# Emptying the first bank of a plain group ahead of the next operands' preparation

## The chip, the cores and the metric

The kernel runs on one core of a Trainium2 chip. The metric is the device time of one execution in microseconds (us). The engines are named as in the profile: PE is TensorE (matmuls), DVE VectorE, ACT ScalarE, SP the engine that issues most DMAs.

## What is computed

One decoder block for 256 tokens of width 2048, in fp32: a mixer and a gated feed-forward network, each with an RMSNorm ahead and a residual sum behind. Cut to what matters:

```python
h = rmsnorm(x, mix_norm_w)
q, k, v, g_out, gk_low, gate_b, gate_c, xc, merge_a, merge_b = split(h @ w_in)
o = rmsnorm(gla_chunked(q, k, v, log_g), gla_norm_w)
y_a = o * silu(g_out)
y_b = gate_b * causal_depthwise_conv(gate_c * xc, conv_w)
x = x + (sigmoid(merge_a) * y_a + sigmoid(merge_b) * y_b) @ w_out
gate, up = split(rmsnorm(x, ffn_norm_w) @ w_gate_up)      # hidden width 5632
x = x + (silu(gate) * up) @ w_down
return rmsnorm(x, final_norm_w)
```

Nearly all of the work is in the products with w_in, w_out, w_gate_up and w_down, whose weights are read once.

## The kernel before

**Split products.** PE multiplies in fp32r. A value is split into hi (rounded) and lo (the rest), and a product is three matmuls: lo of the weights with the activations, hi with their low part, hi with hi (`mm3`, lines 347 to 349 of the profile; the weights are the moving operand there, 128 x 512).

**Pieces.** The weights come in pieces of 512 KB, in the order of one list, `stream`. For each piece `load_piece` issues the DMA into `raw` (5 buffers), then `high` (L238, ACT) writes hi (6 buffers). The lo of a piece, `low` (L243, DVE), is written when the next piece is loaded (`finish_low`). `take` is called for each piece before PE uses it, and loads ahead as far as LOOK = 5 pieces beyond those used. Activations (xh and xl, hh and hl, acth and actl) are split in the same way.

**Two kinds of groups.** A pair of products of the same kind, such as fg4 and fu4 (the gate and the up projection of block 4 of the hidden layer) or gc0 and xc0, is made with seven block products in place of eight (`sevens`). It needs sums of weights: t1 (L259, raw<-y,x) and t3, t2 and t4, which change a tile x in place (L265, x<-x,raw or x<-x,y); each then goes to hi on ACT and to lo on DVE. So such a piece is a chain DVE, ACT, DVE, PE. A pair has five PSUM banks, and at its end the sums v2, v3 and u1 are put together from them on DVE (L424 to L437) and the result goes through a silu on ACT (sg, L1059) and a product on DVE (sg, L1062). The last of these, u1 (L437), reads the bank that the pair's last piece has filled.

The other groups are plain (`eights` for g, gb, ma, mb, wo and the blocks of fg and fu that are not in a pair; `down` for dn). A plain group has two banks, one for each half of the tokens (t = 0 and 1), out of a list of three that is called `lent`. When its last piece has been multiplied for t = 0, that bank is emptied: for g by a silu on ACT (ya, L929), for ma and mb by a sigmoid on ACT and a product on DVE, for wo by a sum on DVE (h, L996), for dn by a sum on DVE (h, L1103), for fg by a silu on ACT (sg8, L1059). The next group needs two of three banks, so its second one is the bank that the group before emptied first. Transposes (trb at L597 from the sg tiles, tr at L583 from h) take a bank of the same list.

**The order of the work.** The pieces of a pair and of plain groups are mixed by rules written out by hand (`gates_list`, `hidden_list`), so a plain group ends somewhere in the midst of a pair. On each engine the instructions stand in the order in which a scheduler puts them, which goes by the order of the program and by what an instruction depends on; an engine works its own list from the front to the back.

Of the kernel before, what the change touches and what calls it, by code (L numbers as in the profile page):

```python
# [12 lines left out]
ALU = mybir.AluOpType  # L13
# [55 lines left out]
PARTS = ((0, 3), (3, 6), (6, 9), (9, 11))  # L69
# [107 lines left out]
def stream_list():  # L177

    pieces = [(p[0], p[3]) for p in piece_list()]
    out = [e for e in pieces if e[0][0] in "kqv"] + gates_list() + [e for e in pieces if e[0] == "wo0"]  # L180
    return out + hidden_list() + down_list()
# [3 lines left out]
def block_kernel(ctx, tc, x, xt, cols_in, gkw_in, gku_in, gnw, conv_w, finw, w_in, w_out, w_gu, w_dn, out):  # L185
    nc = tc.nc
# [12 lines left out]
    def bank(shape, name, tag=None):  # L199

        if tag is None:
            tag = f"b{turn['b'] % turn['of']}"
            turn["b"] += 1
        return psum.tile(shape, F32, tag=tag, name=name)
# [11 lines left out]
    LOOK = 5  # L216
    stream = stream_list()
# [6 lines left out]
    count = {"loaded": 0, "used": 0, "tick": 0}  # L224
    pending = []
    held = {}
# [8 lines left out]
    def high(raw, piece, a=0, b=None):  # L235
        hi, n = piece[0], piece[2]
        ks = slice(a, b or n)
        nc.scalar.copy(hi[:, ks, :], raw[:, ks, :])  # L238

    def low(raw, piece, a=0, b=None):  # L240
        hi, lo, n = piece
        ks = slice(a, b or n)
        nc.vector.tensor_tensor(out=lo[:, ks, :], in0=raw[:, ks, :], in1=hi[:, ks, :].bitcast(F32), op=ALU.subtract)  # L243

    def sum_of(pair, what, q):

        one, two = pair
        if what == "21":
            return fetch(one, 4 * q + 2)
        if what == "22":  # L250
            return fetch(two, 4 * q + 2)
        if what == "11":
            held["y"] = fetch(one, 4 * q, held["pool"], "y")
            return held["y"]
        y = held["y"]
        if what == "t1":
            held["x"] = fetch(two, 4 * q, held["pool"], "x")
            raw = wraw.tile([P, 2, 512], F32, tag="raw", name="raw")
            nc.vector.tensor_tensor(out=raw, in0=y, in1=held["x"], op=ALU.add)  # L259
            return raw  # L260
        x = held["x"]
        if halfway and halfway[-1][0] is x:
            finish_low()
        other = y if what == "t2" else fetch(two if what == "t3" else one, 4 * q + 2)
        nc.vector.tensor_tensor(out=x, in0=x, in1=other, op=ALU.add)  # L265
        return x

    def load_piece():


        i = count["loaded"]
        count["loaded"] += 1
        if i < len(stream):
            key, k0 = stream[i]
            if isinstance(k0, tuple):
                n, w = 2, 512
                raw = sum_of(key, *k0)
                step = n
            else:
                mat, j, n, w = index[(key, k0)]  # L280
                raw = wraw.tile([P, n, w], F32, tag="raw", name="raw")

                step = n // 2 if i < 2 else n
            piece = [whi.tile([P, n, w], F32R, tag="hi", name="hi"), None, n]
            if isinstance(k0, tuple):
                high(raw, piece)
                halfway.append((raw, piece, key, k0))
            else:
                if i < 2:
                    piece[1] = wlo.tile([P, n, w], F32R, tag="lo", name="lo")  # L290
                for a in range(0, n, step):
                    b = a + step
                    if (i, a) in hooks:
                        hooks.pop((i, a))()
                    nc.sync.dma_start(
                        raw[:, a:b, :], mats[mat][j, :, a * w:b * w].rearrange("p (k c) -> p k c", c=w))
                    high(raw, piece, a, b)
                    if i < 2:
                        low(raw, piece, a, b)
                if i < 2:  # L300
                    ready[(key, k0)] = piece
                else:
                    halfway.append((raw, piece, key, k0))
        if len(halfway) > 1 or (halfway and i >= len(stream)):
            finish_low()

    def finish_low():
        raw, piece, key, k0 = halfway.pop(0)
        piece[1] = wlo.tile([P, piece[2], PIECE // piece[2]], F32R, tag="lo", name="lo")
        low(raw, piece)  # L310
        ready[(key, k0)] = piece
# [19 lines left out]
    def one_at_a_time(delay, fn):  # L331

        spaced.append((count["tick"] + delay, fn))

    def take(key, k0):
        while count["loaded"] <= len(stream) and count["loaded"] <= count["used"] + LOOK:
            load_piece()
        return ready.pop((key, k0))

    def used(n=1):  # L340
        count["used"] += n
        for _ in range(n):
            tick()
# [7 lines left out]
    def tok_piece(ps, t, piece, k0, first, last, a):  # L351
        hi, lo, n = piece
        for k in range(n):
            ah, al = a(t, k0 + k)
            mm3(ps, ah, al, hi[:, k, :], lo[:, k, :], first and k == 0, last and k == n - 1)
# [19 lines left out]
    def eights(key, a, done, tags=None):  # L375

        mine = tags or [lent.pop(0) for _ in range(NT)]
        ps = [bank([P, 512], f"{key}_{t}", tag) for t, tag in enumerate(mine)]
        for k0 in range(0, KC, 2):
            piece, _ = yield  # L380
            for t in range(NT):
                tok_piece(ps[t], t, piece, k0, k0 == 0, k0 == KC - 2, a)

                if k0 == KC - 2:
                    done(t, ps[t])
        if tags is None:
            lent.extend(mine)

# [676 lines left out]
    order = hidden_list()  # L1065
# [17 lines left out]
    def hidden_act(part):  # L1083
        def pair(t, k):
            hi, lo = act_of(PARTS[part][0] + k // 4)
            ts = slice(t * P, (t + 1) * P)
            return hi[:, k % 4, ts], lo[:, k % 4, ts]

        return pair

    def down(key):

        part, n = (int(s) for s in key[2:].split("_"))
        cs = slice(DOWN[part][n][0], sum(DOWN[part][n]))
        mine = [lent.pop(0) for _ in range(NT)]
        ps = [bank([P, cs.stop - cs.start], f"{key}_{t}", tag) for t, tag in enumerate(mine)]
        number = sum(e[0] == key for e in order)
        for i in range(number):
            piece, k0 = yield
            for t in range(NT):  # L1100
                tok_piece(ps[t], t, piece, k0, i == 0, i == number - 1, hidden_act(part))
                if i == number - 1:
                    nc.vector.tensor_tensor(out=h[:, t, cs], in0=ps[t], in1=h[:, t, cs], op=ALU.add)  # L1103
        lent.extend(mine)

    def hidden(key):
# [39 lines left out]
    order = down_list()  # L1146
# [15 lines left out]
    for e in order:  # L1162
        key, k0 = e
# [82 lines left out]
```

## Time and profile before

| what | value |
|---|---|
| median of 3 runs | 1505.06 us (1503.34, 1506.04, 1505.06) |
| profiled execution | 1504.77 us, span 1503.1 us |
| granted clock of TensorE | 0.999 |
| PE busy | 1489.3 us, 99% |
| DVE busy | 1277.8 us, 85% |
| ACT busy | 862.9 us, 57% |
| mean of one lo (L243) and one hi (L238) | 1218 ns and 1047 ns |
| HBM | 235 GB/s over the span |

A row of a timeline has the start in us from the span's start, the duration, the engine, the line, the operation, out<-in with the tiles' names, and behind them, in brackets, how long the engine had been idle before and what released it. A row with x2 or more holds several instructions. The durations of matmuls are modelled, and overlap; their starts tell how they follow each other. The page's groups give busy time, the mean of one, and the idle time before; a row of PE's waits has the total, the number and the longest.

### The profile page before, as it was taken

The page shows a single profiled execution, that of the slowest core. Times are in us where ns is not written, and L with a number is a line of the kernel's source. Part 1 is how long each engine was busy: PE and PEld are TensorE (multiplying, and loading weights), DVE is VectorE, ACT ScalarE, POOL GpSimd, SP SyncE. Part 2 cuts the span into 40 slices and gives each one's busy share as a digit, 9 for nine tenths or more (in the row PEclk, how much of TensorE's full clock was granted, in tenths as well). Part 3 has the DMA queues.
Part 4 walks back from the last instruction along what each step waited for, and adds up shares of the span by engine and source line. Part 5 has one row for each costly group of instructions (what it writes and reads, how often), then busy time and mean ns, then how long its engine had stood idle before and what let it go on. Part 6 is the DMA issues. An engine that isn't in the chain of part 4 may idle for free.

```text
span 1503.1 us, 19369 instructions
## 1 busy us (share of the span) xinstructions
PE 1489.3 (99%) x7064; PEld 1243.9 (83%) x7064; DVE 1277.8 (85%) x1283; ACT 862.9 (57%) x977; POOL 37.9 (3%) x60
## 2 busy tenths in 40 slices
PE   9999999999999999999999999999999999999998
PEld 8989988888888888888888888888888788888887
DVE  6775869979979878966689999999999999999975
ACT  7773546655654654654556756655565556565553
POOL 0030000000000000000000000000000000000000
PEclk9999999999999999999999999999999999999999
DMA  9655557876886977786666777777877778777782
GB/s 354 200 170 179 171 170 265 273 230 232 281 259 235 304 227 252 258 264 209 217 220 214 238 246 251 255 261 220 272 238 239 253 263 269 246 263 231 235 287 94
DMA packets 100127, 358.57 MB, mean 239 GB/s; under 512 B 11492, under 2 KB 11620, under 8 KB 99904
## 3 DMA queue, kind: packets, MB, share of 16 engines
q1 hardware_dynamic: 96656, 346.73, 70.8%
q0 software_dynamic: 2800, 8.89, 2.2%
q10 hardware_dynamic: 576, 1.72, 0.3%
q8 instruction: 55, 0.90, 0.2%
q14 instruction: 40, 0.33, 0.1%
HBM read 351.03 MB, written 2.10 MB: 235 GB/s over the span
## 4 chain that ended last, share of the span: by engine, by line
PE 89%; DVE 5%; issue 3%; ACT 2%; DMA 1%; SPq 0%; DVEq 0%; ACTq 0%
PE fg L347 7%; PE fg L349 7%; PE fg L348 7%; PE dn L347 5%; PE dn L349 5%; PE dn L348 5%; PE gc L347 3%; PE gc L348 3%; PE gc L349 3%; DVE lo L243 3%; PE wo L347 2%; PE v L347 2%; PE v L348 2%; PE gb L347 2%; PE gb L349 2%
## 5 line engine op out<-in xcount | busy, mean ns | idle before, releaser
L243 DVE TENSOR_TENSOR lo<-raw,hi 128x1024 fp32r<-128x1024 f32 (+1 forms) x506 | 612.5, 1218 | 109.1 <-ACT hi L238 28.0
L238 ACT CAST hi<-raw 128x1024 fp32r<-128x1024 f32 (+1 forms) x506 | 523.8, 1047 | 270.8 <-PE gb L349 26.4
L238 ACT CAST hi<-x 128x1024 fp32r<-128x1024 f32 x144 | 151.6, 1053 | 276.2 <-DVE x L265 211.0
L243 DVE TENSOR_TENSOR lo<-x,hi 128x1024 fp32r<-128x1024 f32 x144 | 176.2, 1223 | 36.1 <-ACT hi L238 26.1
L347 PE MATMUL dn<-lo,acth 128*128 128x512 f32 (+1 forms) x368 | 140.8, 383 | 1.8 <-DVE h L1103 1.0
L349 PE MATMUL dn<-hi,acth 128*128 128x512 f32 (+1 forms) x368 | 139.9, 380 | 0.0
L348 PE MATMUL dn<-hi,actl 128*128 128x512 f32 (+1 forms) x368 | 139.8, 380 | 0.0
L265 DVE TENSOR_TENSOR x<-x,raw 128x1024 f32<-128x1024 f32 x96 | 117.1, 1220 | 14.7 <-DMA raw<-in_w_in_dram 9.3
L347 PE MATMUL fg<-lo,hh 128*128 128x512 f32 x288 | 112.4, 390 | 0.0
L348 PE MATMUL fg<-hi,hl 128*128 128x512 f32 x288 | 112.2, 389 | 0.0
L349 PE MATMUL fg<-hi,hh 128*128 128x512 f32 x288 | 112.2, 389 | 0.0
L347 PE MATMUL fg<-lo,sh 128*128 128x512 f32 x256 | 101.0, 395 | 0.0
L348 PE MATMUL fg<-hi,sl 128*128 128x512 f32 x256 | 99.9, 390 | 0.0
L349 PE MATMUL fg<-hi,sh 128*128 128x512 f32 x256 | 99.8, 390 | 0.0
L347 PEld LDWEIGHTS dn<-lo,acth 128*128 128x128 f32 x368 | 69.2, 188 | 16.2 <-DVE h L1103 2.3
L349 PEld LDWEIGHTS dn<-hi,acth 128*128 128x128 f32 x368 | 69.2, 188 | 13.3
L348 PEld LDWEIGHTS dn<-hi,actl 128*128 128x128 f32 x368 | 69.3, 188 | 12.9
L347 PEld LDWEIGHTS fg<-lo,hh 128*128 128x128 f32 x288 | 54.1, 188 | 11.8 <-DVE lo L243 0.5
L349 PEld LDWEIGHTS fg<-hi,hh 128*128 128x128 f32 x288 | 54.1, 188 | 11.2
L348 PEld LDWEIGHTS fg<-hi,hl 128*128 128x128 f32 x288 | 54.1, 188 | 11.1
L243 DVE TENSOR_TENSOR lo<-y,hi 128x1024 fp32r<-128x1024 f32 x48 | 58.5, 1219 | 5.4 <-ACT hi L238 2.4
L259 DVE TENSOR_TENSOR raw<-y,x 128x1024 f32<-128x1024 f32 x48 | 58.6, 1220 | 3.0 <-DMA y<-in_w_in_dram 1.5
(247 smaller groups left out, 3068.1 us busy)
## 6 DMA issues: line engine op xcount, KB each, us to landing
raw<-in_w_in_dram SPq DMA_DIRECT2D x254, 512.0 KB, 4.6
raw<-in_w_gu_dram SPq DMA_DIRECT2D x176, 512.0 KB, 4.4
raw<-in_w_dn_dram SPq DMA_DIRECT2D x88, 512.0 KB, 4.5
x<-in_w_gu_dram SPq DMA_DIRECT2D x32, 512.0 KB, 4.9
y<-in_w_gu_dram SPq DMA_DIRECT2D x32, 512.0 KB, 3.8
raw<-in_w_out_dram SPq DMA_DIRECT2D x32, 512.0 KB, 3.7
y<-in_w_in_dram SPq DMA_DIRECT2D x16, 512.0 KB, 4.2
x<-in_w_in_dram SPq DMA_DIRECT2D x16, 512.0 KB, 4.9
```

Source lines behind the costliest of these rows:

```text
L238: nc.scalar.copy(hi[:, ks, :], raw[:, ks, :])
L243: nc.vector.tensor_tensor(out=lo[:, ks, :], in0=raw[:, ks, :], in1=hi[:, ks, :].bitcast(F32), op=ALU.subtract)
L259: nc.vector.tensor_tensor(out=raw, in0=y, in1=held["x"], op=ALU.add)
L265: nc.vector.tensor_tensor(out=x, in0=x, in1=other, op=ALU.add)
L347: nc.tensor.matmul(ps, lhsT=sh, rhs=ml, start=first, stop=False, skip_group_check=onto)
L348: nc.tensor.matmul(ps, lhsT=sl, rhs=mh, start=False, stop=False, skip_group_check=onto)
L349: nc.tensor.matmul(ps, lhsT=sh, rhs=mh, start=False, stop=last, skip_group_check=onto)
```

## The change

The set `ends` holds the place in the stream of the last piece of each plain group: those whose names begin with g or m, v1, wo1 to wo3, the plain fg and fu, and dn but for the last part. There `take` looks 4 pieces ahead in place of 5, so that the load of one piece, its hi, and the lo or the sums that go with it, come one take later, behind the group's emptying in the program. The emptying itself goes through `emptying`: for t = 0 it notes the last instruction on DVE and the last on ACT that the emptying wrote, and the next `take` puts what it loads after these two on their engines (`tc.issue_after`, which fixes an order of issue, and is no wait). v1 is in the set, but its group has no such emptying: there only the shorter look ahead holds. The DMAs of the piece that is put off go with it. The function `down` has its sum in a small function `added` for that.

```diff
+    ends = {}
+    for i, (key, k0) in enumerate(stream):
+        if not isinstance(key, tuple) and (key[0] in "gm" or key == "v1" or key[:2] in ("wo", "fg", "fu", "dn")):
+            ends[key] = i
+    ends = {i for key, i in ends.items() if key != "wo0" and key[:3] != f"dn{len(PARTS) - 1}"}
+
     def take(key, k0):
-        while count["loaded"] <= len(stream) and count["loaded"] <= count["used"] + LOOK:
-            load_piece()
+        look = LOOK - (count["used"] in ends)
+        with ExitStack() as order:
+            for ins in held.pop("emptied", ()):
+                order.enter_context(tc.issue_after(ins))
+            while count["loaded"] <= len(stream) and count["loaded"] <= count["used"] + look:
+                load_piece()
         return ready.pop((key, k0))
+
+    def emptying(done, t, ps):
+        traced = nc.cur_bb.bb.instructions
+        last = traced[-1]
+        done(t, ps)
+        if t == 0:
+            start = next(k for k in reversed(range(len(traced))) if traced[k] is last) + 1
+            new = {i.engine: i for i in traced[start:]}
+            held["emptied"] = [new[e] for e in (mybir.EngineType.DVE, mybir.EngineType.Activation) if e in new]
...
-                    done(t, ps[t])
+                    emptying(done, t, ps[t])
...
+        def added(t, ps):
+            nc.vector.tensor_tensor(out=h[:, t, cs], in0=ps, in1=h[:, t, cs], op=ALU.add)
...
-                    nc.vector.tensor_tensor(out=h[:, t, cs], in0=ps[t], in1=h[:, t, cs], op=ALU.add)
+                    emptying(added, t, ps[t])
```

The lines below the change move down by 19 to 22: L929 becomes L951, L1103 becomes L1122. Each engine has the same instructions as before; the order differs. In the rows below a tile's name ends in a number, which tells buffers of one name apart.

ScalarE at the end of g2, before: three hi stand ahead of the table load and the two silus that empty the banks of g2.

```order
L238 CAST hi_4528<-raw_4526 128x1024
L238 CAST hi_4545<-raw_4544 128x1024
L238 CAST hi_4560<-raw_4558 128x1024
L929 ACT_TABLE_LOAD
L929 ACTIVATE ya_4570<-g2_0_4309,r1_120 128x512
L929 ACTIVATE ya_4570<-g2_1_4310,r1_120 128x512
L238 CAST hi_4581<-raw_4580 128x1024
```

And there in the changed kernel:

```order
L238 CAST hi_4528<-raw_4526 128x1024
L238 CAST hi_4545<-raw_4544 128x1024
L951 ACT_TABLE_LOAD
L951 ACTIVATE ya_4564<-g2_0_4309,r1_120 128x512
L951 ACTIVATE ya_4564<-g2_1_4310,r1_120 128x512
L238 CAST hi_4576<-raw_4574 128x1024
L238 CAST hi_4581<-raw_4580 128x1024
```

One hi has gone from ahead of the emptying to behind it.

VectorE where the pair fg4 ends and fg5 begins, before (fg4_1 is the pair's bank that is filled last; x_8726 is the tile of sums of fg5):

```order
L243 TENSOR_TENSOR lo_8744<-raw_8728,hi_8730 128x1024
L243 TENSOR_TENSOR lo_8757<-raw_8740,hi_8741 128x1024
L265 TENSOR_TENSOR x_8726<-x_8726,raw_8752 128x1024
L437 TENSOR_TENSOR u1_8777<-fg4_1_8112,v2_8116 128x512
L1062 SCALAR_TENSOR_TENSOR sg7_8110<-u1_8777,r2_6320,sg7_8110 128x512
L243 TENSOR_TENSOR lo_8769<-x_8726,hi_8755 128x1024
```

And in the changed kernel:

```order
L243 TENSOR_TENSOR lo_8744<-raw_8728,hi_8730 128x1024
L459 TENSOR_TENSOR u1_8777<-fg4_1_8112,v2_8116 128x512
L243 TENSOR_TENSOR lo_8757<-raw_8740,hi_8741 128x1024
L265 TENSOR_TENSOR x_8726<-x_8726,raw_8752 128x1024
L1084 SCALAR_TENSOR_TENSOR sg7_8110<-u1_8777,r2_6320,sg7_8110 128x512
L243 TENSOR_TENSOR lo_8769<-x_8726,hi_8755 128x1024
```

u1 has moved up past a lo and the first sum x of fg5; the product sg stays where it was.

VectorE where fg7 ends and fg9 begins, before (x_10761 is the tile of sums of fg9):

```order
L243 TENSOR_TENSOR lo_10767<-y_10749,hi_10751 128x1024
L243 TENSOR_TENSOR lo_10779<-raw_10763,hi_10765 128x1024
L265 TENSOR_TENSOR x_10761<-x_10761,raw_10787 128x1024
L243 TENSOR_TENSOR lo_10792<-raw_10775,hi_10776 128x1024
L243 TENSOR_TENSOR lo_10804<-x_10761,hi_10790 128x1024
L437 TENSOR_TENSOR u1_10812<-fg7_1_10138,v2_10142 128x512
L265 TENSOR_TENSOR x_10761<-x_10761,y_10749 128x1024
L1062 SCALAR_TENSOR_TENSOR sg7_10136<-u1_10812,r2_6320,sg7_10136 128x512
```

And in the changed kernel:

```order
L243 TENSOR_TENSOR lo_10767<-y_10749,hi_10751 128x1024
L243 TENSOR_TENSOR lo_10779<-raw_10763,hi_10765 128x1024
L459 TENSOR_TENSOR u1_10812<-fg7_1_10138,v2_10142 128x512
L1084 SCALAR_TENSOR_TENSOR sg7_10136<-u1_10812,r2_6320,sg7_10136 128x512
L243 TENSOR_TENSOR lo_10792<-raw_10775,hi_10776 128x1024
L265 TENSOR_TENSOR x_10761<-x_10761,raw_10787 128x1024
L622 TENSOR_TENSOR actl_10729<-trb_10866,acth_10728 128x4x128
L243 TENSOR_TENSOR lo_10804<-x_10761,hi_10790 128x1024
```

u1, the product sg behind it, the lo of a plain piece and an actl now stand ahead of the lo that belongs to the first sum of fg9; u1, sg and that plain lo also stand ahead of the sum itself.

## Prediction

> **What bounds the kernel now.** I read the page first: busy time, then the groups.
>
> ```profile
> PE 1489.3 (99%) x7064; PEld 1243.9 (83%) x7064; DVE 1277.8 (85%) x1283; ACT 862.9 (57%) x977; POOL 37.9 (3%) x60
> L243 DVE TENSOR_TENSOR lo<-raw,hi 128x1024 fp32r<-128x1024 f32 (+1 forms) x506 | 612.5, 1218 | 109.1 <-ACT hi L238 28.0
> L265 DVE TENSOR_TENSOR x<-x,raw 128x1024 f32<-128x1024 f32 x96 | 117.1, 1220 | 14.7 <-DMA raw<-in_w_in_dram 9.3
> ```
>
> PE is the bound, and only a pause of PE can be won or added. DVE is second, at 85%: it has little room to catch up in the stretches where a pair of products makes its sums (x, L265) beside the lo of every piece. Then the waits of PE:
>
> ```profile
> PE dn L347 <- DVE h L1103: 1.0, 2, 0.5
> PE ma L347 <- ACT ya L929: 0.6, 1, 0.6
> ```
>
> None of PE's waits is larger than some 1 us, and these two are what the change is about: the next group's bank is emptied too late. PE's timeline gives their true size, since starts, not the modelled ends, tell what a pause costs:
>
> ```profile
> 510.46 0.39 PE L348 MATMUL ma<-hi,xl 128*128 128x512 f32 x1
> 510.69 0.39 PE L349 MATMUL ma<-hi,xh 128*128 128x512 f32 x1
> 511.71 0.50 PE L347 MATMUL ma<-lo,xh 128*128 128x512 f32 x1 [0.64 <-ACT ya L929]
> 512.05 0.40 PE L348 MATMUL ma<-hi,xl 128*128 128x512 f32 x1
> ...
> 1173.75 0.39 PE L349 MATMUL dn<-hi,acth 128*128 128x512 f32 x1
> 1174.64 0.50 PE L347 MATMUL dn<-lo,acth 128*128 128x512 f32 x1 [0.50 <-DVE h L1103]
> ...
> 1419.81 0.39 PE L349 MATMUL dn<-hi,acth 128*128 128x512 f32 x1
> 1420.65 0.50 PE L347 MATMUL dn<-lo,acth 128*128 128x512 f32 x1 [0.45 <-DVE h L1103]
> ...
> 1433.49 0.39 PE L349 MATMUL fg<-hi,sh 128*128 128x512 f32 x1
> 1434.80 0.66 PE L597 MATMUL trb<-ident,sg 128*128 128x128 f32 x4 [0.92 <-DVE sg L1062]
> ```
>
> Undisturbed matmuls start 0.23 us apart (510.46, 510.69). Beyond that the three bank waits cost 0.79, 0.66 and 0.61, and about 0.11 more each in the first gap behind (511.71 to 512.05 is 0.34): 0.9, 0.77 and 0.72, together 2.4 us. By the same reading of the timeline the smaller waits for a bank (two at the transposes of h, two in later plain groups) are about 0.2 to 0.3 each: some 1 us. So the change can win 3.4 us at most, of 1503.1.
>
> **The change, place by place.** It adds and removes no instruction: the counts on every engine stay. At the end of a plain group one piece's load, its hi, and the lo or x before it, go behind the emptying of bank 0. Where PE stands far behind the preparation nothing comes of it (the early gates, the plain stretches): there the moved hi and lo have several us until PE uses them. I looked for the places where the margin is under 3 us or a bank wait stands.
>
> *What is won.* At 511.71, ScalarE's timeline:
>
> ```profile
> 508.60 1.05 ACT L238 CAST hi<-raw 128x1024 fp32r<-128x1024 f32 x1 [2.94 <-DMA raw<-in_w_in_dram]
> 509.68 1.28 ACT L929 ACT_TABLE_LOAD   x1
> 510.97 1.26 ACT L929 ACTIVATE ya<-g,r 128x512 f32<-128x512 f32 x2
> ```
>
> A hi waits 2.94 us for its DMA, and table load and ya stand behind it. Now they go ahead and fall into that idle time: the 0.9 goes. The lo behind the moved hi has room. **-0.9.** At wo1 and wo2 the same is done for the transposes of h: their copies out of the bank pass a hi. **-0.6** for the two. At 1174.64 and 1420.65 the 0.77 and 0.72 go; but in each place PE then comes earlier to a transpose that waits for sg (the 1434.80 row: sg came 1.1 us late there, and it hangs on a hi that waits for a DMA, so it does not move forward). That gives it back: **-0.2** at the second. At the first, x and sg of the next pair fall about 1 us behind as well, for the pieces 549 to 553 of the stream, of which the last has 0.2 of room: **+0.3**.
>
> *What is lost.* At the end of a pair its last sum u (L437) reads a bank that PE has just finished. Where a plain group ends near by, u now stands ahead of a lo and of x. VectorE around the end of fg4, and the two times of PE that count there:
>
> ```profile
> 1027.93 1.23 DVE L243 TENSOR_TENSOR lo<-raw,hi 128x1024 fp32r<-128x1024 f32 x1 [0.30 <-ACT hi L238]
> 1029.07 1.22 DVE L265 TENSOR_TENSOR x<-x,raw 128x1024 f32<-128x1024 f32 x1
> 1030.21 0.68 DVE L437 TENSOR_TENSOR u<-fg,v 128x512 f32<-128x512 f32 x1
> 1030.93 0.75 DVE L1062 SCALAR_TENSOR_TENSOR sg<-u,r,sg 128x512 f32<-128x512 f32 x1
> ...
> 1040.97 1.22 DVE L243 TENSOR_TENSOR lo<-x,hi 128x1024 fp32r<-128x1024 f32 x1
> ```
>
> ```profile
> 1028.44 0.39 PE L349 MATMUL fg<-hi,sh 128*128 128x512 f32 x1
> ...
> 1042.26 0.48 PE L347 MATMUL fg<-lo,hh 128*128 128x512 f32 x1
> ```
>
> u can start at 1028.44 + 0.39 = 1028.83, not before. The queue is free at 1027.63 (1027.93 less the 0.30 idle before it), so VectorE stands 1.2 us, where before it soon went on with a lo. Then u 0.68, lo 1.14 (its spacing), and x starts at 1030.6 rather than 1029.07: 1.55 later. From x on it is a chain, x, hi, lo, x, with VectorE full in between, so the lateness stays; sg's place is the same, so u is not won back until it has passed (0.1). The lo at 1040.97 ends at 1042.20, in time by 0.07 before; now at 1043.65 against 1042.26: **+1.4**.
>
> The end of fg7 is the same:
>
> ```profile
> 1275.70 1.22 DVE L265 TENSOR_TENSOR x<-x,raw 128x1024 f32<-128x1024 f32 x1
> ...
> 1279.24 0.68 DVE L437 TENSOR_TENSOR u<-fg,v 128x512 f32<-128x512 f32 x1
> 1280.97 0.74 DVE L1062 SCALAR_TENSOR_TENSOR sg<-u,r,sg 128x512 f32<-128x512 f32 x1
> ...
> 1287.91 1.21 DVE L243 TENSOR_TENSOR lo<-x,hi 128x1024 fp32r<-128x1024 f32 x1
> ```
>
> ```profile
> 1276.86 0.39 PE L349 MATMUL fg<-hi,sh 128*128 128x512 f32 x1
> ...
> 1291.44 0.39 PE L347 MATMUL fg<-lo,hh 128*128 128x512 f32 x1
> ```
>
> u waits until 1276.86 + 0.39 = 1277.25; then u 0.68, sg 0.74 and a lo 1.14 come ahead of x, which starts at 1279.8: 4.1 later. That work no longer stands behind x, so the chain from x on has only its own steps and one lo of another piece in each round: x 1.22, hi 1.05, lo 1.14, lo 1.14, 4.6 from one x to the next. The lo quoted belongs to the third x: 1279.8 + 4.6 + 4.6 + 1.22 + 1.05 + 1.22 = 1292.5 against its use at 1291.44: **+1.1** (1.6 if the pieces before come late too).
>
> At the end of fg9 a hi goes behind sg<-fg (ScalarE), u ahead of a lo and x, and then the emptying of dn2_0 ahead of the lo that x feeds:
>
> ```profile
> 1358.58 1.22 DVE L265 TENSOR_TENSOR x<-x,raw 128x1024 f32<-128x1024 f32 x1
> 1359.72 0.68 DVE L437 TENSOR_TENSOR u<-fg,v 128x512 f32<-128x512 f32 x1
> ...
> 1364.51 1.28 DVE L1103 TENSOR_TENSOR h<-dn,h 128x512 f32<-128x512 f32 x2
> ...
> 1370.97 1.23 DVE L243 TENSOR_TENSOR lo<-x,hi 128x1024 fp32r<-128x1024 f32 x1
> ```
>
> ```profile
> 1372.41 0.40 PE L347 MATMUL fg<-lo,hh 128*128 128x512 f32 x1
> ```
>
> sg<-fg waits for PE until 1355.8 and ends at 1356.4; the hi behind it ends at 1357.4, its lo at 1358.7, u at 1359.3, a lo more at 1360.4: there x starts, 1.8 later. What stands behind is the same work in another order, and I let 0.2 be won back by u, which no longer stands between: the lo at 1370.97 ends at 1373.8 instead of 1372.2, used at 1372.41: **+1.4**.
>
> Two smaller ones. ScalarE at g0, and the first use by PE of the piece that the hi of 229.19 makes:
>
> ```profile
> 229.19 1.05 ACT L238 CAST hi<-raw 128x1024 fp32r<-128x1024 f32 x1
> 230.25 1.28 ACT L929 ACT_TABLE_LOAD   x1
> 231.55 1.27 ACT L929 ACTIVATE ya<-g,r 128x512 f32<-128x512 f32 x2
> ```
>
> ```profile
> 233.78 0.39 PE L347 MATMUL ma<-lo,xh 128*128 128x512 f32 x1
> ```
>
> Table load and ya, 1.28 + 1.27, go ahead of that hi, which then ends at 232.8; on VectorE ya<-ya,o, done at 233.0, stands ahead of its lo, which ends at 234.3: **+0.6** with the semaphore's way. Near 1123 an x and an actl go ahead of a lo with 1.33 of margin, 1.14 + 0.68 against it: **+0.5**.
>
> **Sum**: -0.9 - 0.6 - 0.2 + 0.3 + 1.4 + 1.1 + 1.4 + 0.6 + 0.5 = +3.6 us. The profiled execution took 1504.77 (span 1503.1 and 1.7 around it), 0.3 under the median of the runs, 1505.06. 1504.77 + 3.6 = 1508.4. I sum from the profile, whose rows I used.
>
> A rule bears on the three u's: the Trainium skill, "Perfetto Trace Analysis", section "Per-instruction lifecycle: what the profiler-reported window actually captures", says that VectorE and ScalarE take their queues strictly in order. By it, an u that waits for its bank holds the lo and x behind it, which the 2.94 us row of ScalarE above shows as it happens here (table load and ya begin only when the hi is done). Were it otherwise, the lost terms of the u's would be nothing and the sum -0.3.
>
> **Unknown costs.** The late lo of the three pairs: between 0 (the next x takes the slack of a shorter queue, and PE's other late pieces shift the uses) and 1.55 to 1.8 (the whole lateness of x): I take 1.1 to 1.4, since the lo in question had 0.07 to 2.3 us of room and the chain none to spare. The wins: between 0 (all given back at the next lo or transpose) and -3.4.
>
> **Rivals.**
>
> *Faster.* Only the bank waits go, and PE's lead covers what is moved. -3.4, 1501.4. For it: most margins in the plain stretches are over 4 us, and the bank waits are on PE itself. Against it: the 0.07 at 1042.26. The Trainium skill, "PSUM — Partial Sum Buffer", section "Summary: rules for kernel authors", says to empty banks promptly, which speaks for this case; here the rows of the bank waits agree that a late emptying costs 0.6 to 0.8 each. That is what the page would make of the change. Chance 0.15.
>
> *No change that can be measured* (within 0.2%, 3 us, which is what a measurement of this kernel can tell). The bank waits go, the next wait for sg or lo takes their place, and the u's cost half of what I reckon: -1.5 - 0.2 + 0.3 + 2 + 0.6 = +1.2, about 1506. For it: 1434.80 shows a wait that follows at once; VectorE has 15% idle in all. Against: near the pairs' ends it has none between its rows. Chance 0.37.
>
> *Slower*, the forecast: u at the head of VectorE's queue. It decides from the point where x starts over 1.3 us later than before. Chance 0.48. If the chains delay further pairs, or the late ones bring the x's DMA late in its turn, 1512.
>
> Not doing what it says is hardly possible: the new order shows the emptying ahead.
>
> **Numbers.** Likeliest 1508.4; the forecast's own range is 1506 to 1512. The whole range takes in no change and part of the faster case, 1502.2 to 1511.8. Faster 0.15, same 0.37, slower 0.48.
>
> **What would show it.** Right: PE's waits for h L1122 and for ya L951 (their new lines) gone, no 511.71; new waits of PE for lo L243 of 0.5 us and over behind the ends of fg4, fg7 and fg9, and u on VectorE with about 1 us idle before it, released by PE. Wrong: no such waits and PE's busy end 3 us earlier (faster), or u ahead of x with the lo still in time (same).

## The result, and the profile after

| | before | changed |
|---|---|---|
| median | 1505.56 us (1503.34 to 1508.43, 6 runs) | 1516.89 us (1515.17 to 1517.91, 6 runs) |
| profiled execution, span | 1504.77, 1503.1 us | 1516.16, 1514.5 us |
| granted clock of TensorE | 0.999 | 0.998 |

The ratio is 1.0072 (95% interval 1.006 to 1.0085): 9 to 13 us slower, where the prediction had 3.6 and a range that ended at 1511.8. The page of the changed kernel, busy time and the two groups:

```profile
PE 1493.0 (99%) x7064; PEld 1243.1 (82%) x7064; DVE 1273.5 (84%) x1283; ACT 858.5 (57%) x977; POOL 37.9 (3%) x60
...
L243 DVE TENSOR_TENSOR lo<-raw,hi 128x1024 fp32r<-128x1024 f32 (+1 forms) x506 | 610.7, 1217 | 94.3 <-ACT hi L238 28.3
...
L265 DVE TENSOR_TENSOR x<-x,raw 128x1024 f32<-128x1024 f32 x96 | 117.0, 1218 | 14.8 <-DMA raw<-in_w_in_dram 9.7
```

Work and durations are those of before (a lo 1217 ns against 1218). Only when things happen has changed. The waits of PE:

```profile
PE fg L369 <- DVE lo L243: 3.2, 11, 0.5
PE trb L619 <- DVE sg L1084: 3.1, 3, 1.4
PE gc L369 <- DVE lo L243: 2.2, 2, 1.9
...
PE g L369 <- DVE sb L942: 0.9, 1, 0.9
PE ma L369 <- DVE lo L243: 0.8, 1, 0.8
```

The two waits for a bank that the prediction quoted (h L1103, ya L929) are gone; in their place PE waits for lo, sg and sb. At g2 the gain is there as forecast: ScalarE's table load and silu have gone ahead of the hi, and PE's next bank comes without a pause (before, 0.79 us at 511.71).

```profile
507.56 1.28 ACT L951 ACT_TABLE_LOAD   x1
509.09 0.69 ACT L951 ACTIVATE ya<-g,r 128x512 f32<-128x512 f32 x1 [0.25 <-PE g L371]
```

```profile
512.74 0.39 PE L371 MATMUL ma<-hi,xh 128*128 128x512 f32 x1
512.97 0.39 PE L369 MATMUL ma<-lo,xh 128*128 128x512 f32 x1
```

To find where the time went, I took for each of the 696 pieces of the stream the start of PE's first matmul with it, in the timelines of both kernels, and subtracted: PE's lateness. It moves at a few places only. This table has the step at each place, beside the prediction's term and what the runs further down gave with that end alone.

| place | us in the program before | predicted | measured step | that end alone |
|---|---|---|---|---|
| g0 | 234 | +0.6 | +0.9 | |
| behind mb0 (and g1) | 367 to 385 | 0 | +1.9 | +0.6 (mb0 without g1), within the spread (below) |
| a wait for lo that the lateness covers | 478 | 0 | -0.7 | |
| g2 | 511 | -0.9 | -0.9 | -0.9 |
| behind mb2 | 605 to 625 | 0 | +2.5 | +2.0 |
| wo1, wo2 | 763 to 800 | -0.6 | -0.7 | -0.7 |
| end of fg4 | 1035 to 1046 | +1.4 | +1.4 | +1.5 (dn0_0) |
| dn0_3 | 1123 | +0.5 | +0.2 | |
| dn1_1 to fg7's first pieces | 1175 to 1210 | +0.3 | +0.1 | |
| end of fg7 | 1257 to 1292 | +1.1 | +3.7 | +2.5 (dn1_3) |
| end of fg9 | 1327 to 1375 | +1.4 | +2.8 | +1.5 (fu8) |
| dn2_2 | 1420 to 1436 | -0.2 | -0.3 | |
| sum | | +3.6 | +10.9 | |

10.9 of PE's lateness is what the two profiled executions differ by (11.4) but for some tenths at the end. Four rows, behind mb0, behind mb2, fg7 and fg9, are 8.4 us over their terms together, and the others 1.1 under: that makes the missing 7.3.

The largest single wait is at 374 us. VectorE of the changed kernel at the end of mb0, and further on:

```profile
328.69 0.69 DVE L459 TENSOR_TENSOR u<-gc,v 128x512 f32<-128x512 f32 x1 [0.53 <-PE gc L371]
329.41 0.75 DVE L979 SCALAR_TENSOR_TENSOR u<-gc,r1sq,u 128x512 f32<-128x512 f32 x1
330.74 0.69 DVE L942 TENSOR_TENSOR sb<-sb,mb 128x512 f32<-128x512 f32 x1 [0.58 <-ACT mb L941]
331.35 1.22 DVE L243 TENSOR_TENSOR lo<-x,hi 128x1024 fp32r<-128x1024 f32 x1
332.48 0.68 DVE L942 TENSOR_TENSOR sb<-sb,mb 128x512 f32<-128x512 f32 x1
333.08 1.22 DVE L265 TENSOR_TENSOR x<-x,y 128x1024 f32<-128x1024 f32 x1
...
340.55 1.22 DVE L259 TENSOR_TENSOR raw<-y,x 128x1024 f32<-128x1024 f32 x1 [1.58 <-DMA y<-in_w_in_dram]
...
370.50 1.21 DVE L953 TENSOR_TENSOR ya<-ya,o 128x1024 f32<-128x1024 f32 x1
371.63 1.22 DVE L932 TENSOR_TENSOR sb<-sb,ya 128x1024 f32<-128x1024 f32 x1
372.77 1.21 DVE L243 TENSOR_TENSOR lo<-x,hi 128x1024 fp32r<-128x1024 f32 x1
```

And PE there:

```profile
371.78 0.39 PE L371 MATMUL ma<-hi,xh 128*128 128x512 f32 x1
374.04 0.50 PE L369 MATMUL gc<-lo,sh 128*128 128x512 f32 x1 [1.87 <-DVE lo L243]
```

Two u's and one emptying stand ahead of a lo, and a second emptying ahead of x<-x,y, with 0.53 and 0.58 us of waiting in between. In the kernel before that x<-x,y started at 329.34; here at 333.08. The buffer y is free only then, so SP issues the next y later (330.58 before, 334.32 here), and raw<-y,x waits 1.58 us for it. None of this delays PE at once: its use of the pieces is 2 to 4 us away. The wait of 1.87 us comes 40 us later; whether it is the same loss is what the experiments ask.

### The profile page after: what moved, and what is told of

Same layout as the page of the kernel before. It is cut to its first block, busy times and chain, and to the rows that moved or that the text cites. A ratio compares the mean times of both kernels' runs of the same rounds, so it can differ in the third digit from the quotient of the medians.

```text
span 1514.5 us, 19345 instructions
## 1 busy us (share of the span) xinstructions
PE 1493.0 (99%) x7064; PEld 1243.1 (82%) x7064; DVE 1273.5 (84%) x1283; ACT 858.5 (57%) x977; POOL 37.9 (3%) x60
## 4 chain that ended last, share of the span: by engine, by line
PE 80%; DVE 10%; DMA 4%; issue 4%; ACT 3%; SPq 0%; DVEq 0%; ACTq 0%
PE fg L369 6%; PE fg L371 5%; PE fg L370 5%; DVE lo L243 5%; PE dn L369 4%; PE dn L371 4%; PE dn L370 4%; PE gc L369 3%; PE gc L371 3%; PE gc L370 3%; DVE x L265 3%; ACT hi L238 2%; PE v L369 2%; PE wo L369 2%; PE wo L370 2%
## 5 line engine op out<-in xcount | busy, mean ns | idle before, releaser
L243 DVE TENSOR_TENSOR lo<-raw,hi 128x1024 fp32r<-128x1024 f32 (+1 forms) x506 | 610.7, 1217 | 94.3 <-ACT hi L238 28.3
L238 ACT CAST hi<-raw 128x1024 fp32r<-128x1024 f32 (+1 forms) x506 | 521.9, 1046 | 239.3 <-DMA raw<-in_w_in_dram 22.4
L265 DVE TENSOR_TENSOR x<-x,raw 128x1024 f32<-128x1024 f32 x96 | 117.0, 1218 | 14.8 <-DMA raw<-in_w_in_dram 9.7
L371 PEld LDWEIGHTS fg<-hi,hh 128*128 128x128 f32 x288 | 54.1, 188 | 11.3
L243 DVE TENSOR_TENSOR lo<-y,hi 128x1024 fp32r<-128x1024 f32 x48 | 58.5, 1218 | 4.5 <-ACT hi L238 2.2
```

What stands on the lines that cost most here:

```text
L371: nc.tensor.matmul(ps, lhsT=sh, rhs=mh, start=False, stop=last, skip_group_check=onto)
```

## The experiments

Theories. **Place** (and **lost lead**): a moved row takes from the lead that the preparation has on PE. Where a pair makes its sums VectorE is full, so the lead isn't won back, and PE pays at the next thin margin, however far. **Local** (the prediction's): a place costs what its own next pieces lack. **Late transfer**: the weights' DMAs that start one take later are what costs. **Shorter look ahead**, **holding**: one of the two halves of the change costs as such.

A lateness or a step in the text below is PE's against the profile before, worked out as above. All times are beside runs of the kernel before on the same chip.

**The transfer at its old place.** The fifth piece's DMA is written in the program where it was before; its hi, lo and sums come one take later. VectorE's and ScalarE's order is the changed kernel's. Of the edit only the call is shown; the rest lets `load_piece` use the tile that `fetch_early` has begun to fill.

```diff
             while count["loaded"] <= len(stream) and count["loaded"] <= count["used"] + look:
                 load_piece()
+        if look < LOOK and count["loaded"] < len(stream):
+            fetch_early(*stream[count["loaded"]])
```

> The changed kernel, but where it looks 4 pieces ahead the fifth piece's DMA is still issued at the old place; only its hi, lo and sums come later. The order on VectorE and ScalarE is the changed kernel's, row for row. Queue theory (what costs is u and the emptying ahead of lo and x on VectorE): within 3 us of the changed kernel, 1514 to 1519. Late-transfer theory (what costs is that the piece's DMA starts one take later; the trace of the changed kernel has waits of up to 3.0 us for such a DMA): within 3 us of the kernel before, 1503 to 1508.

Measured: 1515.72 us (1515.30 to 1517.75, 4 runs) beside 1504.53; ratio 1.0071 (1.0055 to 1.0088). That is the time of the changed kernel, but it doesn't rule the late transfer out, because the edit brought no transfer forward. In the trace SP issues all 667 DMAs in the changed kernel's order, and beyond PE's own lateness they start 0.77 us later than before on average, against 0.79 in the changed kernel. So this run is a second execution of the changed kernel's order. The wait for y in the quoted stretch is 0.96 there instead of 1.58, with the same order of instructions and nearly the same time of issue, and PE gains 0.6 less of lateness behind it.

```profile
334.39 0.33 SPq L232 DMA_DIRECT2D y<-in_w_in_dram  x1
```

```profile
339.99 1.23 DVE L259 TENSOR_TENSOR raw<-y,x 128x1024 f32<-128x1024 f32 x1 [0.96 <-DMA y<-in_w_in_dram]
```

**The two halves.** Only the shorter look ahead, and only the holding:

```diff
-            for ins in held.pop("emptied", ()):
-                order.enter_context(tc.issue_after(ins))
+            held.pop("emptied", ())
```

> Only the shorter look ahead at the ends; nothing is held behind the emptying. By the order of its instructions the moves at the end of fg7 and fg9 (v2, u1, sg ahead of lo and x), at dn0_3, dn1_1 and dn2_2 are there, and those at g0, mb0, mb2, g2, wo and fg4 are not. Place theory (each moved row at a pair's sums costs what PE lost there in the changed kernel: fg7 3.7, fg9 2.6, the others +0.2 together): 1511 to 1512. If the shorter look ahead by itself costs (a piece less of lead at 42 ends): as the changed kernel, 1516. If only the holding behind the emptying costs: 1505.

```diff
-        look = LOOK - (count["used"] in ends)
+        look = LOOK
```

> Only the holding of the next loads behind the emptying; the look ahead is 5 throughout. In its order u1 at the end of fg7 and fg9 stands ahead of lo and x as in the changed kernel, with a move at ma0 and one behind mb0, and nothing at g2, wo and fg4. Place theory: fg7 3.7 and fg9 2.6, and 0 to 2 behind mb0: 1511 to 1513. If only the shorter look ahead costs: 1505. If only the holding costs: 1516.

Measured: look ahead alone 1512.16 (1511.48 to 1512.91), ratio 1.0053 (1.0038 to 1.0068); holding alone 1513.51 (1510.54 to 1514.80), ratio 1.0059 (1.0044 to 1.0074), both beside 1504.08. Neither half is the culprit: each is as slow as the places whose rows it moves. In the first, PE is 1 us ahead at 1100 us and loses 3.8 at fg7 and 3.1 at fg9; in the second, 4.4 at the end of gc1's sums (376 us, where the place theory had 0 to 2), 2.8 at fg7 and 3.0 at fg9.

**The groups of the mixer alone.** `ends` and `emptying` only for g, gb, ma, mb and v1.

```diff
+ and (key[0] in "gmv" and key[:2] != "wo")
```

> The change for the groups of the mixer alone (g, gb, ma, mb and v1). Place theory: as the changed kernel up to 700 us, PE 3.6 us late there (g0 0.9, behind mb0 2.0, behind mb2 2.5, less 0.9 at g2 and some 0.8 of waits that the lateness covers), and level from there on: 1508 to 1509. The prediction's terms for these places (0.6 at g0, -0.9 at g2): 1504 to 1505.

Measured: 1507.96 (1505.29 to 1509.18, 10 runs) beside 1504.08; ratio 1.0024 (1.0014 to 1.0034). As the place theory has it, in the total. In its profile PE lost 4.5 us behind mb0, not 1.9, with the same order: raw<-y,x waited longer for y there (the changed kernel's row is the 340.55 above).

```profile
337.41 1.22 DVE L265 TENSOR_TENSOR x<-x,raw 128x1024 f32<-128x1024 f32 x1
341.98 1.23 DVE L259 TENSOR_TENSOR raw<-y,x 128x1024 f32<-128x1024 f32 x1 [3.35 <-DMA y<-in_w_in_dram]
```

```profile
375.48 0.79 PE L369 MATMUL gc<-lo,sh 128*128 128x512 f32 x1 [2.44 <-DVE lo L243]
```

So three executions with the same order there had 0.96, 1.58 and 3.35 us of waiting for y at 340, and 1.3, 1.9 and 4.5 us of lateness gained by PE from 365 to 390.

**More work for VectorE, at two places.** The kernel before, with the lo of one piece written four times: 3.4 us more of VectorE, once where sums begin (piece 127, 328 us) and once where there are none (piece 115, 304 us).

```diff
-        low(raw, piece)
+        for _ in range(4 if (key, k0) == stream[127] else 1):
+            low(raw, piece)
```

> The kernel before, with the lo of one piece (127 of the stream, at 328 us, where a pair's sums begin) written four times: 3.4 us more work for VectorE, nothing else. Lost-lead theory: PE is late by 2 to 3.4 us from about 371 us on. Local theory: the margins of the next pieces are 3.6 to 7 us, so 0.

> The same three extra writes of lo, at piece 115 of the stream (304 us), where the pair before has no more sums to make and the margin is 7.0 us. Lost-lead theory: VectorE has room there and the lead is back before the next sums (324 us): PE late by under 0.3 us at 400 us. If any work for VectorE costs its time in these stretches: 3.4 us late.

Measured, one run each, beside 1504.53: 1510.55 at piece 127 and 1503.91 at piece 115. At 115 the margin (PE's first use of a piece less the end of its lo) falls from 7.0 to 3.4, is 4.9, 5.2 and 6.8 at the next three pieces and 7.0 again at the fourth behind; PE's lateness at 400 us is under 0.1. At 127 it stays gone. VectorE of the kernel before is busy 9.03 of the 14 us from 298 to 312, and 44.70 of the 46 us from 328 to 374. The same work costs nothing or all of itself. Margins in us at some pieces of gc1, from the timelines (piece 126 is ahead of the place):

```
piece (use before)      126 333.1   128 337.1   131 343.9   136 353.5   140 361.6   143 367.1
before                       5.8         3.6         4.6         7.0         5.4         2.9
lo written four times        5.8         0.2         1.1         3.6         1.4         0.1
changed kernel               5.8         2.6         1.9         4.5         3.3         0.8
mixer alone                  5.8         2.6         0.1         2.8         1.6         0.1
changed, less work (below)   5.8         2.6         2.7         5.2         4.8         4.5
```

The 3.4 us are still missing 30 us later (7.0 and 3.6, 5.4 and 1.4), where they reach PE. The cost was 5.9 us by 376, more than the 3.4 that were added: from piece 143 on, the scheduler also put the rows in another order, so only the margins up to there are a clean reading. The total isn't. No row of VectorE, ScalarE or PE waits for a DMA from 328 to 372 us in this run: lead is lost here without a transfer that anything waits for.

**Less work for VectorE between loss and wait.** The changed kernel without three products of the first block's convolution with its taps (352 to 360 us).

```diff
-            later(CONV_AT + n, lambda ...)
+            if i or n > 2:
+                later(CONV_AT + n, lambda ...)
```

> The changed kernel, without three products of the convolution with its taps on VectorE (352 to 360 us, 3.4 us of work; the first block's convolution is left without its taps). Lost-lead theory: the margin that mb0's end took is back by piece 144, and the wait of 1.9 us at 374 us is gone: PE as late at 390 us as at 365 us, 0.5 to 1 us, or less. If PE waits at 374 for the moved rows there alone: the wait stays, 1 us and over.

Measured, one run: 1511.83 us, with 1501.85 for the one run of before beside it and 1516.89 for the changed kernel. The margins are the last row above: the lead is back by piece 140, and PE goes through the place of the 1.87 us wait without a pause:

```profile
371.94 0.39 PE L371 MATMUL ma<-hi,xh 128*128 128x512 f32 x1
372.17 0.39 PE L369 MATMUL gc<-lo,sh 128*128 128x512 f32 x1
```

PE is 1.0 late at 365 us and 0.1 at 390. Not all of the gain in margin comes from the work left out: y was waited for 0.81 us in place of 1.58, so 0.8 of it stands at piece 131 already, ahead of the three products. The transfer run, with 0.96, is the fairer neighbour: 1.4 at piece 143 against 4.5, about 3 of the 3.4 us. Room on VectorE gives the lead back. (At piece 145 the order differs as well; the margins up to 143 stand ahead of that.)

**One end each.** `ends` and `emptying` for a single group. Two of these, mb0 and fu8, were taken first at a granted clock of 0.75 and 0.56 throughout (1858.6 and 2511.3 us) and can't be compared; they were run again.

```diff
+ and (key == "mb0")
```

> Only the end of mb0 (at 328 us) is treated as in the change. Lost-lead theory (the preparation comes about 3 us nearer to PE there and a full VectorE does not win it back until PE meets a thin margin 45 us later): PE 2 to 3 us late from 371 to 385 us on, and nothing late before; 1506 to 1508 in all, since a wait of 0.6 at 478 us that stands in the kernel before is covered. Local theory (the prediction's: a margin of 3.6 us and over behind mb0 covers it): no lateness over 0.3 us, 1503 to 1506.

> As e5, the end of mb0 alone, since the profile of e5 has a granted clock of 0.75 throughout. Lost-lead theory: PE 2 to 5 us late from 365 to 385 us on, where the lead lost at 328 us meets a thin margin, and nothing late before 365 us. Local theory: no lateness over 0.3 us.

mb0: 1507.27 beside 1504.88. PE gained 1.8 us of lateness at 372, gave back 1.1 by 381 (a wait of the kernel before is covered) and kept 0.6: between the theories (2 to 5 us late, or at most 0.3), and no more than the spread of this place: in seven profiles whose order there is that of before (three ends, five ends, the fill at piece 115, dn0_0, dn1_3, mb2, fu8), PE gained 0 to 1.1 us at 376, where the margin of the kernel before is 0.06. So the time of this run doesn't show what mb0 costs PE. The margins show what it takes. At piece 131 the kernel before has 4.57, and mb0 alone, less work, the transfer run, the changed kernel and the mixer alone have 3.06, 2.67, 2.51, 1.90 and 0.12. They waited for y 0.41, 0.81, 0.96, 1.58 and 3.35 us: each lost 1.1 us for the moved rows and its wait for y on top, one for one. In mb0 alone 1.0 of its 1.5 is still missing at piece 143 (1.9 against 2.9). That the rest of the 1.9 in the table comes from g1's moved rows (ya<-ya,o and sb<-sb,ya ahead of the lo, at 370.50) is argued, not shown.

> The change at the end of mb2 alone (599 us). In its order raw<-y,x and the emptying of mb2 stand ahead of an x and a lo. Place theory: what PE lost behind mb2 in the changed kernel, 2.5 us from 605 to 627, of which 1.1 is the wait for sb behind a raw<-y,x that waits for y's DMA: 1.5 to 2.8 us late by 630, nothing before. Prediction (margins of 4 to 6 us cover it): 0.

mb2: 1507.58, beside one run of before at 1501.85. PE 0.3 late at 600, 2.4 at 625, +2.0 (at this place the spread is smaller: 0.8 in the fill at piece 115, about 0.3 and less in the others). VectorE before, and with mb2's end moved, and PE:

```profile
600.12 1.23 DVE L265 TENSOR_TENSOR x<-x,raw 128x1024 f32<-128x1024 f32 x1
601.26 1.22 DVE L243 TENSOR_TENSOR lo<-raw,hi 128x1024 fp32r<-128x1024 f32 x1
602.45 1.23 DVE L259 TENSOR_TENSOR raw<-y,x 128x1024 f32<-128x1024 f32 x1
```

```profile
603.39 1.23 DVE L259 TENSOR_TENSOR raw<-y,x 128x1024 f32<-128x1024 f32 x1 [3.55 <-DMA y<-in_w_in_dram]
604.53 0.68 DVE L945 TENSOR_TENSOR sb<-sb,mb 128x512 f32<-128x512 f32 x1
605.13 1.22 DVE L265 TENSOR_TENSOR x<-x,raw 128x1024 f32<-128x1024 f32 x1
```

```profile
605.27 0.50 PE L369 MATMUL g<-lo,xh 128*128 128x512 f32 x1 [0.36 <-DVE sb L945]
```

raw<-y,x now stands ahead of x, of sb and of a lo. It waits 3.55 us for y, and all of them with it; the emptying that was to come sooner comes late, and PE waits for just that bank. The transfer itself isn't late: SP issues this y at 597.44, and at 597.68 in the kernel before. The less-work run has this end's rows moved too and lost only 0.3 here, with a wait of 2.73 us: its pieces came with 1 us more of margin (5.9 against 4.8 at piece 257).

> The change at the end of dn0_0 alone (1010 us). In the order, u1 at the end of fg4 moves ahead of a lo and x, 20 us behind, and nothing else of weight. Place theory: PE is in time until 1035 us and 1.3 to 1.4 us late by 1047, in three steps (in the changed kernel 0.2, 0.5 and 0.6): the prediction's term for fg4, 1.4. If the lateness that PE brought along in the changed kernel, or the shorter look ahead, made that cost: 0 to 0.3.

dn0_0: u1 ahead at the end of fg4, by itself. The one run took 1505.09 beside 1504.88; PE's lateness goes from 0.5 at 1030 to 2.0 at 1047, +1.5 (it is won back further on at waits that the profile of before has and this one hasn't, below). From 1023 to 1050 us no row of VectorE, ScalarE or PE waits for a DMA: at fg4 the order alone makes the cost.

```profile
1029.45 0.69 DVE L462 TENSOR_TENSOR u<-fg,v 128x512 f32<-128x512 f32 x1 [0.41 <-PE fg L371]
1030.05 1.22 DVE L243 TENSOR_TENSOR lo<-raw,hi 128x1024 fp32r<-128x1024 f32 x1
1031.18 1.22 DVE L265 TENSOR_TENSOR x<-x,raw 128x1024 f32<-128x1024 f32 x1
```

```profile
1039.56 0.50 PE L369 MATMUL fg<-lo,sh 128*128 128x512 f32 x1 [0.32 <-DVE lo L243]
1044.25 0.50 PE L369 MATMUL fg<-lo,hh 128*128 128x512 f32 x1 [0.31 <-DVE lo L243]
```

> The change at the end of dn1_3 alone (1237 us). All moved rows at the ends of fg7 and fg9 come with it. Place theory: what PE lost there in the changed kernel, 3.7 at 1257 to 1300 and 2.6 at 1350 to 1384, comes from this one end, most of it 20 to 140 us behind it: 1510 to 1511, and nothing late before 1250. The prediction's terms there (1.1 and 1.4): 1507. If each of the 42 ends costs its own small share: 1505.

dn1_3: 1509.69 (1507.05 to 1513.05, 7 runs), ratio 1.0032 (1.0021 to 1.0044). One end of the 38 that the set holds (42, where an expectation has it, is a miscount) makes 3 to 7 of the 9 to 13 us. PE loses 2.5 at fg7 and 2.1 at fg9, 20 to 140 us behind the end that was changed, since the scheduler's order moves there too.

> The change at the end of fu8 alone (1320 us). It brings the moved rows at the end of fg9, 40 us behind, and none at fg7. Place theory: 1.5 to 2.6 us late by 1385, in steps of 0.4 to 0.6 at the pieces of fg10 from 1364 on, and nothing before 1320. If what cost at fg9 in the changed kernel was lead lost already at fg7: under 1.

> As e14, the end of fu8 alone, since the profile of e14 has a granted clock of 0.56 throughout. Place theory: 1.5 to 2.6 us late by 1385, in steps of 0.4 to 0.6 at the pieces of fg10 from 1364 on, and nothing before 1320. If what cost at fg9 in the changed kernel was lead lost already at fg7: under 1.

fu8: 1507.12 beside one run of before at 1504.72. PE loses 1.5 from 1364 to 1376 (0.5, 0.45, 0.6), and from 1327 to 1362 nothing (2.1 late, then 2.0). That is the lower end of what the place theory had, and the prediction's 1.4. The changed kernel gains 1.2 more from 1327 to 1362 (8.46 to 9.64 late): there the pieces came with less lead. The margin of the lo used at 1345.5 is 7.1 in the kernel before, 3.3 with fu8's end alone, 1.3 in the changed kernel; fu8's own order takes 3.8 of it. That what is missing from fg7 on takes the last 2.0 is argued: dn1_3's end alone, which loses at fg7 too, has 3.5 there.

**The ends that gained.** The change at g2, wo1 and wo2, and at these with dn1_1 and dn2_2:

```diff
+ and (key in ("g2", "wo1", "wo2", "dn1_1", "dn2_2"))
```

> The change at g2, wo1 and wo2 alone, the three ends where the changed kernel gained. Place theory: -0.9 at g2 and -0.6 to -0.7 at the transposes of h, no loss: 1503 to 1504 against 1505, 1.5 to 1.6 us less in the profile, which the times can hardly tell. If each end costs lead: 1505 to 1507.

> The change at the five ends where PE waited 0.4 us and over for a bank before and the order moves little besides: g2, wo1, wo2, dn1_1 and dn2_2. Place theory: -0.9 at g2, -0.6 at wo1 and wo2, and -0.8 and -0.7 at dn1_1 and dn2_2: 3.0 us less, 1501 to 1502 beside 1504 to 1505. The prediction's reading that the last two are given back at the transpose that waits for sg: 1.5 us less, 1503.

Measured: three ends 1503.05 (1501.37 to 1506.07, 10 runs) beside 1504.08, ratio 0.9989 (0.9980 to 0.9999); five ends 1502.53 (1501.50 to 1504.99, 11 runs) beside 1504.88, ratio 0.9987 (0.9978 to 0.9996). Five ends are faster than the kernel before, by 0.6 to 3.3 us, and so than both. In the profile of the five, dn1_1 wins 0.8 and the next transpose takes it back, as the prediction had it:

```profile
1185.22 0.66 PE L622 MATMUL trb<-ident,sg 128*128 128x128 f32 x4 [0.75 <-DVE sg L1087]
...
1431.55 0.66 PE L622 MATMUL trb<-ident,sg 128*128 128x128 f32 x4 [0.48 <-DVE sg L1087]
```

## Why the prediction was wrong

**Right: the sign, the mechanism, and seven of its nine terms to 0.3 us.** u1 and the emptying at the head of VectorE's queue hold lo and x. At fg4 u waits 0.56 us for PE's bank in the changed kernel, the lo and x behind it, and x starts 1.54 us later than PE's lateness explains (the prediction: 1.55). VectorE isn't full from there on, as the prediction had it: in the kernel before it stands 1.19 us for a hi at 1036.28. The lateness stays all the same, since each step of the chain waits for the one ahead. Of the seven, the agreement at g0 may be luck (below).

```profile
1031.80 0.69 DVE L459 TENSOR_TENSOR u<-fg,v 128x512 f32<-128x512 f32 x1 [0.56 <-PE fg L371]
1032.41 1.22 DVE L243 TENSOR_TENSOR lo<-raw,hi 128x1024 fp32r<-128x1024 f32 x1
1033.54 1.22 DVE L265 TENSOR_TENSOR x<-x,raw 128x1024 f32<-128x1024 f32 x1
...
1045.31 1.22 DVE L243 TENSOR_TENSOR lo<-x,hi 128x1024 fp32r<-128x1024 f32 x1
```

```profile
1046.59 0.50 PE L369 MATMUL fg<-lo,hh 128*128 128x512 f32 x1 [0.32 <-DVE lo L243]
```

The Trainium skill, "Perfetto Trace Analysis", section "Per-instruction lifecycle: what the profiler-reported window actually captures", has VectorE take its queue strictly in order, and these rows agree: lo and x start only behind the u that waited 0.56 us. The Trainium skill, "PSUM — Partial Sum Buffer", section "Summary: rules for kernel authors", says to empty banks promptly. Emptying sooner at five ends was 2 us faster, and at all 38 it was 11 us slower; the measurement decides.

**Wrong: the step "Where PE stands far behind the preparation nothing comes of it".** I looked for places where a margin was under 3 us, and set all others to nothing. A margin isn't a cover that stands at one place; it is a stock. What the end of mb0 took at 328 (2.0 to 2.7 us in the changed kernel, with 3 to 7 in stock) wasn't there at 367, since VectorE had next to no idle time to win it back in: the fill at piece 127 stayed lost for 30 us, the fill at 115 was made up in 8, and with 3.4 us less work in between the wait of 1.87 us was gone. The row behind mb0 (predicted 0, measured 1.9) is this step. At mb2 (predicted 0, measured 2.5) it failed nearer by: the margin of piece 259, 4 us behind the moved rows, went from 4.7 to 0.1, because the moved raw<-y,x brought its wait for y ahead of them. The part of fg9 beyond 1.4 goes with this step as far as its pieces came with less lead, which is argued.

**Wrong in size: fg7, 1.1 against 3.7.** I reckoned the chain from u1 on as if the pieces came into it with the lead that they had before. Two things had taken from it: dn1_3's end, and a copy on ScalarE that had moved ahead of a hi and waits there for PE, which I had put under "several us until PE uses them":

```profile
1253.98 0.59 ACT L437 COPY v<-fg 128x512 f32<-128x512 f32 x1 [1.33 <-PE fg L371]
1255.13 1.05 ACT L238 CAST hi<-x 128x1024 fp32r<-128x1024 f32 x1 [0.56 <-DVE x L265]
```

dn1_3 alone, without that copy's move, costs 2.5; the look-ahead half, with it, 3.8. From 1241 to 1266 us the four profiles with the copy's move (changed, transfer run, look ahead, less work) lose 0.8 to 1.2 us, and the two without it (dn1_3, holding) nothing: about 1 us is the copy's.

**Without a term in the prediction: the wait for y.** It named a late DMA of x only as the case that leads to 1512. At mb0 there is a loop: a later x<-x,y frees y later, SP issues its DMA later (334.32 against 330.58), and raw<-y,x waits at the head of VectorE's queue. I had counted instructions on VectorE and ScalarE and not the queue on SP that hangs on them. At mb2 y's DMA is issued as early as before; there raw<-y,x has moved ahead of other rows, and its wait (3.55 us with that end alone) holds them.

**Rows that were chance.** The wait at 1434.80 of the profile before (1.1 us), on which I hung that the gain at dn2_2 is given back, is in that execution only: in six profiles in which nothing near was changed (the mixer alone, three ends, both fills, dn0_0, mb2) PE comes 0.9 to 1.2 us earlier there. The steps behind 1430 in my table are uncertain by that much. That the gain is given back at the transposes is shown at dn1_1; at dn2_2 it is likely, by the 0.48 of the row above. At g0 it is the other way round: in three kernels whose order there is that of before (dn0_0, mb0, the fill at 127) PE waits 0.63, 1.03 and 1.15 us for a bank at 233 us, which the profile before doesn't, and loses 0.7 to 1.2. The wait for lo that I forecast is there in the changed kernel (0.76 us at 234.47), but what the end of g0 costs beside an average execution of before isn't shown. And the wait at g2 is missing in two of these three (dn0_0 and mb0), which come 0.7 to 1.0 us earlier there: the gain of 0.9 is that of an execution that had the wait.

**The rivals.** "Only the bank waits go" was right for three ends and wrong for the rest, and "waits for sg take their place" right at dn1_1: neither was the whole.

**Open.** What each of the rows moved behind g1 costs, apart from mb0's, wasn't tried alone. The late transfer is ruled out at fg4 alone. At fg7 ScalarE of the changed kernel waits 1.63 and 2.93 us for pieces (at 1251.59 and 1273.20; before, 2.34 at 1264.95), and the DMAs there start 2.5 us later on average than PE's lateness explains; no run has tried what that costs. Why the scheduler's order moves rows 20 to 140 us behind a changed end can't be read from the traces.

## What to carry to other kernels

When an edit holds back work of an engine that feeds the bound one, don't ask what margin stands at that place, but what the smallest margin is from there to the next stretch in which the feeding engine has idle time: up to there a microsecond that is lost stays lost. Take the benefit end by end: five ends of 38 held the gains, and one end some two fifths of the loss (4.8 of 11.3 us, 3 to 7 by its interval). Read the order of the whole program after such an edit, not only around it, and run the queues of the transfers along with those of the engines.

## What the hardware showed that was not expected

The transfer of y (512 KB) was issued at nearly the same time in three profiles with the same order of instructions around it: 334.32 in the changed kernel, 334.39 with the transfer at its old place, 333.98 in the mixer alone. What waits for it went on at 340.55, 339.99 and 341.98: 6.2, 5.6 and 8.0 us after the issue. The median from issue to landing on the changed kernel's page is less:

```profile
y<-in_w_in_dram SPq DMA_DIRECT2D x16, 512.0 KB, 4.8
```

```profile
333.98 0.33 SPq L232 DMA_DIRECT2D y<-in_w_in_dram  x1
```

In the kernel before y is issued at 330.58, ahead of six small transfers (u<-u, from 331.52 on), and lands 4.0 us later; in these three it is issued behind the six. That they hold it up isn't shown: in the fill at 127 y stands behind them too and landed 4.3 us after its issue.

With PE's step at 376 (0 to 1.1 us with one and the same order), one execution tells nothing of a single end that is worth less than 1 us.
